# Seven block products in place of eight in three of four SwiGLU layers, and the whole state-space preparation beside the fourth

## Chip, cores and metric

The kernel runs on one core of one Trainium2 chip. The metric is the device time of one execution in microseconds (us), and the median of several executions is compared. Engines are named as in the profile: PE is TensorE's matmuls, PEld its weight loads, DVE VectorE, ACT ScalarE, POOL GpSimd, SP SyncE, which here only issues transfers.

## The reference

A trunk of two layers, each made of SwiGLU, token mixing, SwiGLU, runs over 640 tokens (512 latent, 128 context) with a model width of 1024. The token mixing of layer 0 is attention beside RWKV-7, that of layer 1 is a bidirectional S5. All of it is float32.

```python
D_MODEL, D_FF, DEPTH = 1024, 2816, 2
def swiglu(h, w1, w3, w2):
    return (jax.nn.silu(h @ w1) * (h @ w3)) @ w2
def run_trunk(x, mods, P, ctx):
    for l in range(DEPTH):
        h = modulated_in(x, P['norm_pre'][l, 0], m[:, 0])
        f = swiglu(h, P['ffn_w1'][l, 0], P['ffn_w3'][l, 0], P['ffn_w2'][l, 0])
        x = residual_out(x, f, P['norm_post'][l, 0], m[:, 0], 0.5)
        ...  # token mixing: attention and RWKV-7 (l = 0), S5 (l = 1)
        h = modulated_in(x, P['norm_pre'][l, 2], m[:, 2])
        f = swiglu(h, P['ffn_w1'][l, 1], P['ffn_w3'][l, 1], P['ffn_w2'][l, 1])
        x = residual_out(x, f, P['norm_post'][l, 2], m[:, 2], 0.5)
def modulated_in(x, gain, m):
    return rms_norm(x, gain) * (1 + m[:, None, 1]) + m[:, None, 0]
def residual_out(x, y, gain, m, weight):
    return x + weight * m[:, None, 2] * rms_norm(y, gain)
```

S5 also needs tables that depend on its parameters alone (powers of the poles, injection, read-out and Toeplitz matrices); computing them is the state-space preparation.

## The kernel before

Activations are held transposed: features on the partitions (8 tiles of 128), tokens along the row, in two halves of 320. Every float32 product is made of three matmuls on rounded operands: high weights by high activations, high weights by low activations, low weights by high activations (`mm3`, L439 to L441). So each weight tile is split on the chip into `whi` (ACT, L411) and `wlo = w - whi` (DVE, L412) after its load, and each activation tile into a high and a low part (`split`, L363 and L364).

There are four SwiGLU layers, named (layer, place): (0,0), (0,2), (1,0) and (1,2). Each runs `ffn`. Its 22 tiles of 128 hidden features go in six blocks (`FBLOCKS`: 4, 4, 4, 4, 2 and 4 tiles). Per block, the up part forms h @ w1 and h @ w3 for each tile and half (24 matmuls of 128x320 each), applies the gate on ACT and DVE (`th` L478 and L479, `g` L481) and splits the result into `gh` and `gl`; the down part then adds the block's share of all eight output tiles to `y` (L530, L532). In the first and the last block the two halves go one after the other, with their weights split twice, so that the norm of one half runs beside the matmuls of the other.

Between sublayers stand `post_norm` (sum of squares over the tiles, `ms` L335, `rr` on POOL L336, `diag` L340, a broadcast `ps_rb` L341, then `yr` L390 and `x` L393 on DVE) and the next `pre_norm` (the same chain, then `xr` L354 on DVE, `hh` L356 on ACT, `hl` L357 on DVE). For half 0 both are issued after its last down matmul; for half 1 the pre-norm waits until the next sublayer has begun (`flush`).

The preparation (`s5_prep`, 61 jobs) is put between the tiles of two SwiGLU layers as background work. A job of `s5_slice` loads its inputs over POOL's queue, makes twelve DVE products of 128x256 (L1488 to L1490, L1506 to L1508), lets PE transpose or multiply them, and stores the result over POOL's queue. The division is this:

```python
cut = 21 + 5 * 3
bg = {(0, 2): prep[:cut], (1, 0): prep[cut:]}
```

The order of the instructions of each engine is fixed when the kernel is built, by a scheduler that goes by the program's order and raised priorities; each engine then runs its list in order. PSUM has eight banks: three of a ring, one half of a wide tile that serves as every fourth of that ring, and four others.

## Time and profile before

| | us |
|---|---|
| median of 3 runs | 3202.66 (3195.01 to 3205.19) |
| the profiled execution, its own time | 3197.65 |
| span of that profile, first to last instruction | 3195.9 |
| PE busy in the span | 2949.9 |
| DVE, ACT, POOL busy | 1849.7, 1183.1, 711.3 |
| mean granted TensorE clock, share of 2.4 GHz | 0.949 |

A busy time is the sum of an engine's instructions. The views used below are the busy time by stretch (us from the span's start, per engine, with the number of instructions, then the granted clock), the list of an engine's instructions in order of time, and the groups of equal instructions.

### The profile page before, as it was taken

How to read it: one execution, taken by the hardware profiler on the slowest of the kernel's cores; microseconds unless marked ns; L12 is line 12 of the kernel's file. 1: busy time of each engine (PE TensorE's matmuls, PEld its weight loads, DVE VectorE, ACT ScalarE, POOL GpSimd, SP SyncE). 2: the span in 40 equal slices, each digit the busy share in tenths (PEclk: the TensorE clock that was granted, in tenths of full speed). 3: DMA queues.
4: the chain of work that ended last, by engine and by line, in shares of the span. 5: the costliest groups of instructions: out<-in, count | busy, mean ns of one | idle time of the engine just before them, and what ended most of it. 6: DMA issues, size and time to landing. Idle time of an engine off the chain costs nothing.

```text
span 3195.9 us, 57300 instructions
## 1 busy us (share of the span) xinstructions
PE 2949.9 (92%) x23107; PEld 2758.9 (86%) x23107; DVE 1849.7 (58%) x3775; ACT 1183.1 (37%) x2443; POOL 711.3 (22%) x844
## 2 busy tenths in 40 slices
PE   7999998997888788999999999999987699999998
PEld 6999998985666567999999989999986599999998
DVE  5433348524646654864675876665678846533346
ACT  4422235423444534533333542222452245422223
POOL 1000004024312201533231322232224624000002
PEclk8999999997788998999999999999988899999998
DMA  6433335541111107345444454453469653432223
GB/s 227 139 130 121 106 106 181 173 162 49 22 33 31 26 15 208 113 151 159 139 145 127 141 171 146 145 160 105 140 159 253 237 172 104 160 108 77 70 90 112
DMA packets 372302, 408.55 MB, mean 128 GB/s; under 512 B 75465, under 2 KB 338438, under 8 KB 371782
## 3 DMA queue, kind: packets, MB, share of 16 engines
q1 hardware_dynamic: 357542, 365.93, 37.1%
q0 software_dynamic: 14496, 38.97, 4.0%
q8 instruction: 182, 2.98, 0.4%
q14 instruction: 82, 0.67, 0.1%
HBM read 358.79 MB, written 44.86 MB: 126 GB/s over the span
## 4 chain that ended last, share of the span: by engine, by line
PE 79%; DVE 8%; DMA 4%; POOL 3%; ACT 2%; issue 2%; SPq 1%; POOLq 0%; DVEq 0%; ACTq 0%
PE ps_h L439 10%; PE ps_h L440 10%; PE ps_h L441 10%; PE ps_wide L439 6%; PE ps_wide L440 6%; PE ps_wide L441 6%; PE ps_y L439 5%; PE ps_y L440 5%; PE ps_y L441 5%; PE ps_wide L274 2%; DVE s5x L1633 1%; PE ps_in L439 1%; PE ps_in L441 1%; PE ps_in L440 1%; PE ps_n L84 1%
## 5 line engine op out<-in xcount | busy, mean ns | idle before, releaser
L411 ACT CAST whi<-w 128x1024 fp32r<-128x1024 f32 (+2 forms) x576 | 483.1, 846 | 852.9 <-PE ps_h L440 285.0
L412 DVE TENSOR_TENSOR wlo<-w,whi 128x1024 fp32r<-128x1024 f32 (+2 forms) x574 | 574.8, 1007 | 383.6 <-ACT whi L411 374.6
L439 PE MATMUL ps_h<-hh,whi 128*128 128x320 f32 x2112 | 658.2, 312 | 6.8 <-ACT whi L411 2.7
L440 PE MATMUL ps_h<-hl,whi 128*128 128x320 f32 x2112 | 657.3, 311 | 0.3 <-DVE hl L357 0.3
L441 PE MATMUL ps_h<-hh,wlo 128*128 128x320 f32 x2112 | 655.9, 311 | 0.0
L439 PEld LDWEIGHTS ps_h<-hh,whi 128*128 128x128 f32 x2112 | 399.3, 189 | 13.4 <-ACT whi L411 4.6
L440 PEld LDWEIGHTS ps_h<-hl,whi 128*128 128x128 f32 x2112 | 398.8, 189 | 2.8 <-issue 1.5
L441 PEld LDWEIGHTS ps_h<-hh,wlo 128*128 128x128 f32 x2112 | 398.6, 189 | 1.0 <-issue 0.8
L440 PE MATMUL ps_y<-gl,whi 128*128 128x320 f32 x1056 | 325.9, 310 | 0.0
L441 PE MATMUL ps_y<-gh,wlo 128*128 128x320 f32 x1056 | 325.4, 310 | 0.0
L439 PE MATMUL ps_y<-gh,whi 128*128 128x320 f32 x1056 | 323.5, 311 | 1.4 <-ACT y L530 1.3
L439 PE MATMUL ps_wide<-hh,whi 128*128 128x320 f32 x912 | 288.0, 316 | 7.3 <-ACT hh L363 4.4
L440 PE MATMUL ps_wide<-hl,whi 128*128 128x320 f32 x912 | 285.7, 313 | 0.7 <-DVE hl L357 0.7
L441 PE MATMUL ps_wide<-hh,wlo 128*128 128x320 f32 x912 | 284.7, 312 | 0.4 <-DVE wlo L412 0.4
L373 POOL TENSOR_TENSOR ssy<-ssy,sq 128x320 f32<-128x320 f32 x84 | 94.0, 1119 | 562.9 <-ACT sq L372 560.5
L439 PEld LDWEIGHTS ps_y<-gh,whi 128*128 128x128 f32 x1056 | 197.0, 188 | 6.7 <-ACT y L530 2.5
L440 PEld LDWEIGHTS ps_y<-gl,whi 128*128 128x128 f32 x1056 | 198.2, 188 | 0.9 <-issue 0.5
L441 PEld LDWEIGHTS ps_y<-gh,wlo 128*128 128x128 f32 x1056 | 198.0, 188 | 1.1 <-issue 0.8
L439 PEld LDWEIGHTS ps_wide<-hh,whi 128*128 128x128 f32 x912 | 173.6, 190 | 14.5 <-issue 5.3
L481 DVE SCALAR_TENSOR_TENSOR g<-th,ps_h 128x320 f32<-128x320 f32 x159 | 77.1, 485 | 175.1 <-PE ps_h L441 174.7
L440 PEld LDWEIGHTS ps_wide<-hl,whi 128*128 128x128 f32 x912 | 173.1, 190 | 3.3 <-issue 1.4
L441 PEld LDWEIGHTS ps_wide<-hh,wlo 128*128 128x128 f32 x912 | 172.9, 190 | 0.9 <-DVE wlo L412 0.6
(465 smaller groups left out, 5595.4 us busy)
## 6 DMA issues: line engine op xcount, KB each, us to landing
w<-in_ffn_w_dram SPq DMA_DIRECT2D x120, 1024.0 KB
ada_w<-in_ada_w_dram SPq DMA_DIRECT2D x72, 1024.0 KB
w<-in_ffn_w_dram SPq DMA_DIRECT2D x112, 512.0 KB
w<-in_ab_w_in_dram SPq DMA_DIRECT2D x14, 1024.0 KB
s5cd<-s_work POOLq DMA_DIRECT2D x128, 64.0 KB, 2.5
s5bd<-s_st POOLq DMA_DIRECT2D x32, 256.0 KB, 3.6
s5bt<-s5bd SPq DMA_DIRECT2D x32, 256.0 KB
w<-in_s_w_out_dram SPq DMA_DIRECT2D x8, 1024.0 KB
```

Source lines behind the costliest of these rows:

```text
L84: i = self.nc.tensor.matmul(**p).ins
L274: nc.tensor.matmul(ps[32 * g:32 * g + 32, :256], self.sc[:, 2 * t + k, :], w[:, k, g * 256:g * 256 + 256], start=(t + k == 0), stop=(2 * t ...
L373: nc.gpsimd.tensor_tensor(ss, ss, sq, op=OP.add)
L411: a = self.nc.scalar.copy(hi[:, :kt], s)
L412: v = (eng or self.nc.vector).tensor_tensor(lo[:, :kt], s, hi[:, :kt].bitcast(F32), op=OP.subtract)
L439: nc.tensor.matmul(o, hi[:, k], ah[k][half], start=(k == 0), stop=False)
L440: nc.tensor.matmul(o, hi[:, k], al[k][half], start=False, stop=False)
L441: self.last[0] = nc.tensor.matmul(o, lo[:, k], ah[k][half], start=False, stop=(k == kt - 1))
L481: nc.vector.scalar_tensor_tensor(g, t, 0.5, p3[:, :HALF], op0=OP.mult, op1=OP.mult)
L1633: V.tensor_tensor(dst, dst, t1, op=OP.add)
```

## The change

In (0,0), (1,0) and (1,2) the up part of all blocks but the first goes by seven block products. Two hidden tiles and two token halves make a product of 2x2 blocks with the contraction (8 tiles) halved, which takes eight block products in plain form; Winograd's form needs seven (12 matmuls each), of sums and differences of blocks. The sums on the activation side (`t1`, `t2`, `t4`, and half 1's first four tiles overwritten) are made once per layer by `block_inputs`; those on the weight side are made for each pair of tiles and each of w1 and w3, in float32 on POOL, by `sums` in `block_products`, and each of the seven weight blocks (128x512) is split on ACT and DVE. The products are combined on DVE from PSUM. A layer has 9 such pairs with two jobs each, so 54 jobs in all. The blocks become 4, 4, 4, 4, 4 and 2 tiles (`SBLOCKS`); half 1's down part of the last two blocks is joined. Since the new tiles need room, `x` is stored to DRAM before block 1 and loaded again in the last block. All 61 preparation jobs go to (0,2), which stays as it was otherwise.

```diff
+SBLOCKS = ((0, 4), (4, 8), (8, 12), (12, 16), (16, 20), (20, 22))
+    def block_inputs(self):
...
+        for k in range(4):
+            u, a = tmp(), tmp()
+            G(u, f(b12[1][k]), f(b11[1][k]), op=OP.subtract)
+            V(a, f(b12[0][k]), f(b11[0][k]), op=OP.subtract)
+            V(a, a, u, op=OP.add)
+            self.split(t1[0][k], t1[1][k], a)
...
+        return {1: b11, 2: b21, 3: b22, 4: t4, 5: t1, 6: t2, 7: b12}
+    def block_products(self, jobs, moving, pool):
...
+        def split2(m, *parts):
...
+                nc.scalar.copy(h, src)
+                v = nc.vector.tensor_tensor(l, src, h.bitcast(F32), op=OP.subtract)
...
+        def weights(m, stage):
+            if stage == 0:
...
+                def sums():
+                    G(s1, A(1, 0), A(1, 1), op=OP.add)
+                    G(A(1, 0), A(0, 0), A(1, 0), op=OP.subtract)
+                    G(A(0, 0), s1, A(0, 0), op=OP.subtract)
+                split2(m, (1, A(0, 0), sums), (6, A(0, 0), None))
+            elif stage == 1:
+                A = m["A"]
+                split2(m, (2, A(0, 1), lambda: G(A(0, 1), A(0, 1), A(0, 0), op=OP.subtract)), (5, m["s1"], None))
+                split2(m, (7, A(1, 0), None))
+            else:
+                A = m["A"]
+                split2(m, (4, A(1, 1), None), (3, A(0, 1), None))
...
+            if stage == 0:
+                m["X"], m["Y"] = self.ps("ps_x"), self.ps("ps_z")
+                x = prod(m, 1, m["X"], True, False)
...
+                nc.scalar.copy(m["p1"], x)
+                z = prod(m, 6, m["Y"], True, False)
...
+                V(m["u2"], m["p1"], z, op=OP.add)
+            elif stage == 1:
+                m["take"](0, prod(m, 2, m["X"], False, True))
+                m["W"] = self.ps("ps_w5")
+                w = prod(m, 5, m["W"], True, False)
+                z = prod(m, 7, m["Y"], False, False)
...
+            else:
+                z = prod(m, 4, m["Y"], False, True)
...
+                w = prod(m, 3, m["W"], False, True)
...
+                split_early(M[i + 1], 0)
+                split_early(m, 2)
+                split_early(M[i + 1], 1)
+                products(M[i + 1], 0)
+                products(m, 2)
+                products(M[i + 1], 1)
...
+        seven = not bg
+        self.g = self.open("g", 8 if seven else 10)
...
+            if seven and bi == 1:
+                self.spill_x()
+                self.close("res")
+                moving, pool = self.block_inputs(), self.open("blkt")
...
-        cut = 21 + 5 * 3
-        bg = {(0, 2): prep[:cut], (1, 0): prep[cut:]}
+        bg = {(0, 2): prep}
```

Three places in the order of the instructions show it. (Line numbers of the changed kernel are its own: L394 there is L393 before.)

DVE, at the passage from (0,2) to (1,0): `gl` is the last of (0,2), `ms` and `diag` belong to the pre-norm of half 0 of (1,0), and `xr` is the first product of that norm. Before:

```order
L364 TENSOR_TENSOR gl<-g,gh 128x320
L335 TENSOR_SCALAR ms<-ps_ms 128x3
L340 TENSOR_SCALAR diag<-ident,rr 128x128 x2
L340 TENSOR_SCALAR diag<-ident,rr 64x64
L532 TENSOR_TENSOR y_1_12951<-y_1_12951,ps_wide 128x320
L532 TENSOR_TENSOR y_1_12953<-y_1_12953,ps_y 128x320
L412 TENSOR_TENSOR wlo<-w,whi 128x512
L532 TENSOR_TENSOR y_1_12955<-y_1_12955,ps_y 128x320
L412 TENSOR_TENSOR wlo<-w,whi 128x512
L354 SCALAR_TENSOR_TENSOR xr<-x,mods_12946,ps_rb 128x320 x4
```

The last twelve rows up to the same `xr` now (`s_work` and `s_bc` are tiles of the preparation):

```order
L1677 TENSOR_TENSOR s_work<-s_bc,s_lp 128x256
L1676 TENSOR_TENSOR s_work<-s_bc,s_lp 128x256
L1678 TENSOR_TENSOR s_work<-s_work 128x256
L1677 TENSOR_TENSOR s_work<-s_bc,s_lp 128x256
L1678 TENSOR_TENSOR s_work<-s_work 128x256
L1694 TENSOR_TENSOR s_work<-s_bc,s_lp 128x2x16x8
L341 TENSOR_SCALAR diag<-ident,rr 128x128 x2
L1695 TENSOR_TENSOR s_work<-s_bc,s_lp 128x2x16x8
L341 TENSOR_SCALAR diag<-ident,rr 64x64
L1694 TENSOR_TENSOR s_work<-s_bc,s_lp 128x2x16x8
L1696 TENSOR_TENSOR s_work<-s_work 128x256
L1695 TENSOR_TENSOR s_work<-s_bc,s_lp 128x2x16x8
```

Between (0,2)'s last `gl` and the fourth `gl` of (1,0), DVE has 84 instructions before; now it has the same 84 and 101 of the preparation among them. Between the last `gl` of the last block's half 0 and that of its half 1 it has 56 before, now these and 49 of the preparation.

DVE, in the up part of block 2 of (0,0): before, each tile and half takes `th`, `g` and `gl`, and a few weight splits fall between.

```order
L479 SCALAR_TENSOR_TENSOR th<-th,ps_h_3881 128x320
L481 SCALAR_TENSOR_TENSOR g<-th,ps_wide 128x320
L364 TENSOR_TENSOR gl<-g,gh 128x320
L412 TENSOR_TENSOR wlo<-w,whi 128x256
L479 SCALAR_TENSOR_TENSOR th<-th,ps_h_3937 128x320
L481 SCALAR_TENSOR_TENSOR g<-th,ps_h_3938 128x320
```

Now (in a middle block of the same layer; `blk_p`, `blk_u`, `blk_v` and `blk_c` are partial sums of the products, `blk_g` the gate):

```order
L549 TENSOR_TENSOR blk_u<-blk_p,ps_wide 128x320
L503 TENSOR_TENSOR wlo<-w,whi 128x512 x4
L503 TENSOR_TENSOR wlo<-blk_s,whi 128x512
L634 SCALAR_TENSOR_TENSOR blk_g<-blk_g,ps_x 128x320
L556 TENSOR_TENSOR blk_v<-blk_p,ps_wide 128x320
L503 TENSOR_TENSOR wlo<-w,whi 128x512
L557 TENSOR_TENSOR blk_v<-blk_v,ps_w_4244 128x320
L634 SCALAR_TENSOR_TENSOR blk_g<-blk_g,blk_v 128x320
L549 TENSOR_TENSOR blk_u<-blk_p,ps_z 128x320
```

A job has seven splits and five sums that were not there, and its splits take in 3584 columns where two plain tiles took 2048.

POOL, in the same blocks: before it had no work there but the small sums of the modulation; now one job after the other has four sums of 128x512, of which this is one job and the next one's first sum.

```order
L515 TENSOR_TENSOR blk_s<-w 128x512
L516 TENSOR_TENSOR w<-w 128x4x128
L517 TENSOR_TENSOR w<-blk_s,w 128x4x128
L522 TENSOR_TENSOR w<-w 128x4x128
L515 TENSOR_TENSOR blk_s<-w 128x512
```

Over the whole program PE's matmul instructions go from 19,505 to 18,857, all of the difference 128x320; DVE's instructions go from 3,777 to 4,413 and POOL's from 849 to 1,098.

## Rows read from the trace of the kernel before

**Rows 1.** The page: span, and busy time of each engine.

```profile
span 3195.9 us, 57300 instructions
PE 2949.9 (92%) x23107; PEld 2758.9 (86%) x23107; DVE 1849.7 (58%) x3775; ACT 1183.1 (37%) x2443; POOL 711.3 (22%) x844
```

**Rows 2.** Busy time by stretch: in (0,2), at its end, after it, in (1,2).

```profile
core 0: us, PE busy (x) PEld busy (x) DVE busy (x) ACT busy (x) POOL busy (x), PEclk, DMA share, GB/s
1760.00:1840.00 80.00, 80.00 (x550) 79.44 (x549) 69.35 (x129) 42.84 (x78) 29.03 (x27) 1.00 0.42 131
1840.00:1920.00 80.00, 73.94 (x504) 71.17 (x503) 57.22 (x125) 38.76 (x84) 15.48 (x25) 0.96 0.54 170
2880.00:2960.00 80.00, 80.00 (x548) 80.00 (x547) 31.68 (x54) 18.76 (x31) 0.00 (x0) 1.00 0.20 63
```

**Rows 3.** PE in order of time in (0,0): first and last of 36 matmuls.

```profile
469.76 0.31 PE L439 MATMUL ps_h<-hh,whi 128*128 128x320 f32 x1
...
474.90 0.31 PE L441 MATMUL ps_y<-gh,wlo 128*128 128x320 f32 x1
```

**Rows 4.** DVE in order of time; the `gl` that end groups of four.

```profile
1705.35 0.48 DVE L364 TENSOR_TENSOR gl<-g,gh 128x320 fp32r<-128x320 f32 x1
...
1748.76 0.48 DVE L364 TENSOR_TENSOR gl<-g,gh 128x320 fp32r<-128x320 f32 x1
...
1792.66 0.48 DVE L364 TENSOR_TENSOR gl<-g,gh 128x320 fp32r<-128x320 f32 x1
...
1839.61 1.11 DVE L364 TENSOR_TENSOR gl<-g,gh 128x320 fp32r<-128x320 f32 x1 [0.53 <-ACT gh L363]
...
1894.92 0.48 DVE L364 TENSOR_TENSOR gl<-g,gh 128x320 fp32r<-128x320 f32 x1
```

**Rows 5.** DVE in order of time, back to back: start, us, engine, line.

```profile
1796.88 0.48 DVE L532 TENSOR_TENSOR y<-y,ps_y 128x320 f32<-128x320 f32 x1
1797.27 0.68 DVE L412 TENSOR_TENSOR wlo<-w,whi 128x512 fp32r<-128x512 f32 x1
1797.88 0.48 DVE L532 TENSOR_TENSOR y<-y,ps_y 128x320 f32<-128x320 f32 x1
...
1848.52 0.42 DVE L1488 TENSOR_TENSOR s_work<-s_bc,s_lp 128x256 f32<-128x256 f32 x1
1848.86 0.42 DVE L1489 TENSOR_TENSOR s_work<-s_bc,s_lp 128x256 f32<-128x256 f32 x1
1849.19 0.60 DVE L1506 TENSOR_TENSOR s_work<-s_bc,s_lp 128x256 f32<-128x256 f32 x1
1849.63 0.62 DVE L1507 TENSOR_TENSOR s_work<-s_bc,s_lp 128x256 f32<-128x256 f32 x1
```

**Rows 6.** Groups of DVE and POOL: count, busy, mean ns, idle before.

```profile
L1488 DVE TENSOR_TENSOR s_work<-s_bc,s_lp 128x256 f32<-128x256 f32 x64 | 27.0, 421 | 17.6 <-DMA s_bc<-s5bc 14.9 <-DMA s5cd<-s_work 1.7 <-PE ps_s5b L1493 0.4
L857 POOL TENSOR_TENSOR rope<-att_q,k_cos 128x512 f32<-128x512 f32 x4 | 5.1, 1272 | 10.2 <-ACT att_q L794 10.2
L1848 POOL TENSOR_TENSOR s5z<-hh,hl 128x320 f32<-128x320 f32 x16 | 15.2, 950 | 36.4 <-DVE glu L1850 36.4
```

**Rows 7.** DVE and POOL side by side in the S5 scan, in order of time.

```profile
2473.10 0.81 DVE L1633 TENSOR_TENSOR s5x<-s5x,sj 128x640 f32<-128x640 f32 x1
2473.83 1.91 DVE L1632 TENSOR_TENSOR sj<-sj,sj 128x640 f32<-128x640 f32 x1
...
2473.16 1.90 POOL L1628 TENSOR_TENSOR sj<-s5x,s_a 128x656 f32<-128x656 f32 x1
```

**Rows 8.** PE at the passage from (0,0) to (0,1): waits over 1 us.

```profile
554.83 0.63 PE L439 MATMUL ps_in<-hh,whi 128*128 128x320 f32 x1 [8.19 <-ACT pm L767]
570.43 1.81 PE L341 MATMUL ps_rb<-diag,ones 128*128 128x128 f32 x6 [2.04 <-DVE diag L340]
573.52 0.90 PE L439 MATMUL ps_in<-hh,whi 128*128 128x320 f32 x2 [1.29 <-ACT hh L356]
```

**Rows 9.** Transfers of `x`: queue, count, KB each, median us from issue to landing.

```profile
xd<-x POOLq DMA_DIRECT2D x2, 2560.0 KB, 8.9
```

**Rows 10.** Busy time by stretch at the passage from (0,0), columns as in rows 2.

```profile
550.00:555.00 5.00, 0.17 (x1) 0.17 (x2) 5.00 (x14) 2.13 (x7) 3.74 (x3) 0.50 1.03 304
570.00:575.00 5.00, 3.24 (x10) 2.46 (x10) 3.46 (x14) 2.28 (x8) 0.28 (x2) 0.50 0.61 210
```

More of the change, by code (lines that the diff above doesn't have):

```diff
@@ L482, in up, with up_pairs, gate, close @@
             self.split(gh[half], gl[half], g)
+        def up_pairs(f0, gh, gl):
+            jobs = []
+            for p in range(len(gh) // 2):
+                c = slice((f0 + 2 * p) * 128, (f0 + 2 * p + 2) * 128)
+                ts = {}
+                def gate(n, v, ts=ts):
+                    t = ts[n] = pool.tile([128, HALF], F32, name="blk_g", bufs=5)
+                    nc.scalar.activation(t, v, AF.Tanh, scale=0.5)
+                    nc.vector.scalar_tensor_tensor(t, t, 1.0, v, op0=OP.add, op1=OP.mult)
+                def close(n, v, ts=ts, p=p):
+                    t = ts[n]
+                    nc.vector.scalar_tensor_tensor(t, t, 0.5, v, op0=OP.mult, op1=OP.mult)
+                    self.split(gh[2 * p + n // 2][n % 2], gl[2 * p + n // 2][n % 2], t)
+                for w, take in ((w1, gate), (w3, close)):
+                    jobs.append((lambda w=w, c=c: self.wload(w[:, c], KT, 256), take))
+            return self.block_products(jobs, moving, pool)
         bg, slots = list(bg), FBLOCKS[-1][0] - FBLOCKS[0][1]
@@ L494, in background @@
             slots -= 1
[L496 removed]
+        blocks = SBLOCKS if seven else FBLOCKS
+        kept = None
+        for bi, (f0, f1) in enumerate(blocks):
             nb = f1 - f0
[L498 to L500 removed]
+            gh, gl = [[[] for _ in range(nb)] for _ in range(2)]
+            for g, tag in ((gh, "gh"), (gl, "gl")):
+                for _ in range(2):
+                    for i in range(nb):
+                        g[i].append(self.g.tile([128, HALF], F32R, name=tag, tag=tag))
+            first, last = bi == 0, bi == len(blocks) - 1
+            keep = seven and bi == len(blocks) - 2
             ssy = [None, None]
@@ L505, in ffn @@
                 ssy = [self.small.tile([128, HALF], F32, name=f"ssy{h}", bufs=1) for h in range(2)]
-            for hs in (((0,), (1,)) if first or last else ((0, 1),)):
-                for i in range(nb):
+            if seven and bi == 1:
+                self.spill_x()
+                self.close("res")
+                moving, pool = self.block_inputs(), self.open("blkt")
+            if seven and not first:
+                for n, _ in enumerate(up_pairs(f0, gh, gl)):
+                    if n and not last:
+                        background()
+            if seven and last:
+                self.close("blkt", "blk")
+                self.res = self.open("res", 1, "right")
+                self.new_x()
+                for half in range(2):
+                    c = slice(half * HALF, (half + 1) * HALF)
+                    nc.gpsimd.dma_start(self.xt[:, :, c], self.xd[:, :, c])
+            for hs in ((0,),) if keep else ((0,), (1,)) if first or last else ((0, 1),):
+                if kept and hs == (1,):
+                    f0, nb, gh, gl = kept[0], f1 - kept[0], kept[1] + gh, kept[2] + gl
+                for i in range(nb if first or not seven else 0):
                     with ExitStack() as c:
@@ L1898, in run @@
                 self.ffn(l, j, on_half, fill, bg.get((l, j), ()))
-                if prep and (l, j) == (1, 0):
+                if prep and (l, j) == (0, 2):
                     self.close("s5k")
```

78 lines of the change are left out of this document (73 added, 5 removed).

## The prediction

> **What bounds the kernel now.** I read the page first: PE is busy 2949.9 us of a span of 3195.9, DVE 1849.7, POOL 711.3 [rows 1]. Then the stretches: inside the SwiGLU layers PE has no idle time at all, and in (1,2) DVE needs only 31.68 of 80 us and POOL nothing [rows 2]. A matmul is listed with 0.31 us because they are pipelined; what counts is the pitch, (474.90 - 469.76) / 35 = 0.147 us [rows 3]. So there a matmul that is not issued returns 0.147 us, as long as no other engine becomes the bound. Two other readings matter. In the last part of (0,2) DVE is busy 69.35 and POOL 29.03 of 80 us and PE still never waits; in the stretch after it, with the passage to (1,0), PE is down to 73.94 [rows 2]. Other engines may be loaded far within a layer, and are the bound at a passage, where PE waits for the norms.
>
> **Matmuls removed.** 54 jobs with 84 matmuls in place of 96 are 648 fewer, which is the count in the order too. 648 x 0.147 = **-95 us**. PE itself gets nothing new to do.
>
> **The up parts of the block products.** Prices by the distance of one start to the next: a DVE product of 128x320 takes 0.40 us, a split of 128x512 0.61 (1796.88, 1797.27, 1797.88) [rows 5]. Four jobs, a block of four tiles, have 28 splits (17.1 us), 20 sums, 16 gate products and 8 low parts (44 x 0.40 = 17.6): 34.7 us of DVE. POOL has 16 sums at 1.27 us, by the row of the same size (5.1 us for four) [rows 6]: 20.3. PE needs 336 x 0.147 = 49.4 us. Each engine alone fits. But the two do not run freely side by side. In the S5 scan a DVE product of 128x640 with both operands in SBUF takes 0.81 us; the next begins at 2473.83 while POOL's runs until 2475.06, and ends at 2475.74, after 1.91 us [rows 7]: it waited until POOL was done and then took its usual time. 28 + 18 of the DVE instructions here have both operands in SBUF; the others read PSUM. If DVE and POOL took turns throughout, an up part would take 34.7 + 20.3 = 55.0 us, 5.6 more than PE, and 54 jobs 13.5 x 5.6 = 76 us. The other end is 0: the down part that follows has 28 us of matmuls and only 8 x 0.61 + 16 x 0.40 = 11.3 us of DVE, the order places the next block's first splits and POOL sums in it, and so the whole block asks for 66.3 of 77.6 us. The nearest row is the stretch in (0,2): 69.35 + 29.03 = 98 us of DVE and POOL in 80 without a wait of PE [rows 2]. That is a heavier load than here, but with looser dates. In the new form a PSUM bank is written again 24 matmuls (3.5 us) after its last product, so a DVE queue held up by two or three POOL sums is felt. I take **+20 us** (0.4 a job), bounds 0 and 76.
>
> The Trainium skill (SBUF — State Buffer, "Who interferes with whom") gives that waiting as a rule: a VectorE instruction with two SBUF inputs and a GpSimd instruction that reads SBUF share a port pair, held for the whole instruction. Rows 7 agree, with 1.91 us against 0.81. By the rule taken in full the sum ends at the first rival's time below; the row of (0,2) speaks for less.
>
> **The preparation beside (0,2).** PE does the same small products as before, elsewhere; DVE is what counts. A product of the preparation costs 0.34 us, one that reads in steps 0.44 (1848.52, 1848.86; 1849.19, 1849.63) [rows 5]. Between the last `gl` of (0,2) and the fourth of (1,0) stand the same 84 instructions as before and 101 of the preparation: 61 x 0.34 + 32 x 0.44 + 8 small ones = 36 us. Before, that stretch lasted from 1792.66 to 1839.61, 47 us [rows 4]; the 84 take about 37 (44 of 128x320, 8 splits of 128x512, 8 of double size, 24 smaller), so 10 us of idle time can take up a part: +26. The stretch ahead of it lasted 43.9 us (1748.76 to 1792.66) with some 30 us of work, and gets 49 more, 17 us: +3. The one after (to 1894.92) lasted 55, loses 17 instructions of the preparation, and gains 26 of the activation sums: 0. The one before both (1705.35 to 1748.76) stays inside its 43: 0. The stall has a place: the first matmul of (1,0) waits for `hh`, which waits for `xr`, and ahead of `xr` DVE now has 27 us of its list after the last `gl`, where PE has only half 1's down part, 96 x 0.147 = 14 us. So PE should wait some 15 us there, and about as much again within block 0. DVE in order also waits for the loads of the preparation (17.6 us in 64 cases before [rows 6], 0.3 us each). I take **+33 us**. Bounds: 24, if the preparation's DVE work comes into idle time after all, and 45, if every slice waits for its load and TensorE's clock is at 0.50 after the wait, as in the stretches from 550 and 570 [rows 10].
>
> **The activation sums.** Per layer 48 DVE products (19 us) and 8 on POOL at up to 0.95 [rows 6], beside the 576 matmuls (85 us) of block 0. They fit, closely in (1,2), where the second half's norm falls into the same 42 us. **+3 us**, 0 to 10. The store of `x` ahead of them takes about 9 us [rows 9] under the same block.
>
> **The last block.** Half 0's norms had 288 matmuls of half 1 as cover (42 us), now 144 (21 us). Ahead of the next sublayer's first matmul DVE has, beside `yr`, `x` and `xr`, eight `y` sums and eight splits of 128x768 (about 0.9 us each, by 0.61 for 512): some 20 us, and with the waits for `ms`, `rr` and `ps_rb` about 29 us after half 0's last product. PE would wait 8 to 10 us there. But it loses as much now, later: 8.19 + 2.04 + 1.29 us and a spell at a clock of 0.50, at the passage from (0,0), before half 1 can begin [rows 8, 10]; with half 0 later, half 1's norm is ready when its turn comes. **0**, from -8 to +15 for both passages. After (1,2) nothing follows but the output. The load of `x`, half of 2560 KB in half of 8.9 us [rows 9], begins when the last product is done and is needed some 15 us later: hidden, else 5 us a layer, inside that bound.
>
> **The sum.** 3197.65 (the profiled execution's own time) - 95 + 20 + 33 + 3 + 0 = 3158.65. The median of the runs shown is 5.0 us above that execution, so **3164 us**.
>
> **The rivals.** The forecast, a gain of 20 to 60 us, has a chance of 0.48.
> *DVE and POOL take turns in the up parts.* All 76 us are paid: 3202.66 - 95 + 76 + 33 + 3 = 3220, slower. It decides from 1.1 us of PE wait per job (59 us of 95 - 33 - 3). For it speak rows 7; against it the stretch in (0,2) and the work that lies in the down parts. 0.15.
> *Nothing is paid in the up parts* and the preparation costs its lower bound: 3202.66 - 95 + 24 = 3132. For it speaks the same stretch of (0,2). 0.25.
> *The passage costs twice as much.* PE's list there has the preparation's transposes between half 1's down part and the first product of (1,0), each waiting for DVE, which waits for loads issued by POOL behind other waits; such a ring costs by its latencies, not by its work. 70 us in place of 33: 3202.66 - 95 + 20 + 70 + 3 = 3201, no change. Against it: with 45 instructions of the preparation after 1839.61 DVE waited little (55 us for some 43 of work) [rows 4]. 0.12.
> That the matmuls are not saved can't be: the order has them.
>
> **The range.** From 3124 (no up part cost, 24 for the preparation, 8 gained at the passages) to 3226 (the lock in full and a little of the passages). Beyond it, both up parts and passages at their upper bounds would give 3252. For the forecast alone: 3143 to 3183. Faster by over 0.3% (10 us, about what three runs of this kernel can tell): 0.48 + 0.25 = 0.73; within 0.3%: 0.12; slower: 0.15.
>
> **What would show it.** Right: (0,0), (1,0) and (1,2) shorter by about 25 us each (216 x 0.147 = 32 less 7), with waits of PE under 1 us at a time in the up parts; at the passage from (0,2) to (1,0) a PE wait of 10 us or more ended by `hh`, with DVE busy without a gap; POOL and DVE sums stretched to about twice in the up parts. Wrong: waits of PE on `ps_w`, `ps_z` or on weight splits of over 1 us per job (then the first rival), or a passage without a wait (then the second); or PE waits on weight loads, since an up part now frees a load buffer later, which no row here prices.

## The result, and the profile after

The changed kernel is slower: 3242.64 us (median of four, 3236.74 to 3244.68) against 3198.84 for the kernel before beside it, a ratio of 1.0137, 95% interval 1.0122 to 1.0152, or 44 us. The forecast was 3164, a gain, with a range to 3226. 95 us of matmuls went, so 139 us were lost elsewhere, not the forecast's 56.

First the page of the changed kernel, the lines of [rows 1]:

```profile
span 3241.1 us, 57517 instructions
PE 2903.3 (90%) x22459; PEld 2693.9 (83%) x22459; DVE 2205.1 (68%) x4411; ACT 1309.0 (40%) x2791; POOL 1081.9 (33%) x1093
```

PE is busy 47 us less, and the span is 45 us longer: PE waits 92 us more. That is two thirds of the 139 us. The rest is that PE's busy time fell by 47 us and not by 95: the mean granted clock fell from 0.949 to 0.928, and after its waits PE works for a while at 0.50, the lower of its two levels (1.2 GHz), where one matmul follows the other after 0.267 us (six steps from 496.24 to 497.84) and not after 0.147. An estimate, from PE's busy time and clock in every 20 us of both traces: PE was busy at the lower level for some 227 us before and 326 now, and the 99 us more are worth 99 x (1 - 0.147 / 0.267) = 45 us.

Busy time by stretch, with the columns of [rows 2]:

```profile
1760.00:1840.00 80.00, 72.65 (x554) 67.93 (x552) 77.89 (x152) 41.36 (x92) 48.98 (x61) 0.98 0.57 171
1840.00:1920.00 80.00, 56.54 (x386) 49.28 (x386) 71.60 (x163) 27.25 (x67) 47.58 (x72) 0.75 0.51 152
2880.00:2960.00 80.00, 78.95 (x564) 76.54 (x563) 54.62 (x93) 29.76 (x60) 27.09 (x21) 1.00 0.35 113
2960.00:3040.00 80.00, 80.00 (x548) 80.00 (x547) 56.97 (x101) 29.51 (x57) 24.65 (x17) 1.00 0.25 80
```

In the middle blocks of (1,2) PE has hardly a gap, and 548 matmuls in 80 us are still 0.146 us each. Most of what is lost is lost at the edges of the layers: at the end of (0,2) and after it PE is busy 72.65 and 56.54 us where it had 80.00 and 73.94, with the clock at 0.75 in place of 0.96. The stages, by the first product that the trace of each kernel shows in a bank of the sublayer (it can be a few us late; the kernels of the last four columns come below):

| us | before | changed | prep alone | plain last block | wide ring | last form |
|---|---|---|---|---|---|---|
| (0,0) from | 42.5 | 49.1 | 43.2 | 49.6 | 42.9 | 42.9 |
| (0,1) from | 530.7 | 528.3 | 531.4 | 521.9 | 531.1 | 516.6 |
| (0,2) from | 1299.6 | 1305.2 | 1297.0 | 1287.5 | 1302.3 | 1282.1 |
| (1,0) from | 1809.0 | 1855.9 | 1848.8 | 1840.5 | 1851.4 | 1838.4 |
| (1,1) from | 2331.5 | 2381.8 | 2382.6 | 2363.8 | 2343.8 | 2313.6 |
| (1,2) from | 2694.0 | 2754.9 | 2745.7 | 2729.1 | 2711.0 | 2676.3 |
| end | 3195.9 | 3241.1 | 3247.5 | 3214.5 | 3214.1 | 3159.5 |

Read as differences, the changed kernel starts 6.6 us late, gains 9.0 in (0,0) where 31.8 were taken out (216 x 0.147), loses 8.0 in (0,1), 41.3 in (0,2) and 10.6 in (1,1), and gains 15.7 in (1,2). (1,0) takes 3.4 more, with 31.8 us of matmuls and the work of 25 jobs taken out. One trace does not fix such a figure to a few us: (0,1), which no kernel here changes, took from 765.5 to 776.9 in these six, and from 760.4 to 780.0 in all the traces of this case.

The passage from (0,2) to (1,0), PE in order of time, some of its waits:

```profile
1835.05 0.44 PE L1681 MATMUL ps_s5b<-ident,s_work 128*128 128x128 f32 x2 [2.44 <-ACT s_t L1719]
1841.57 0.59 PE L1715 MATMUL ps_s5k<-s_work,s_bb 128*32 128x112 f32 x4 [2.27 <-DVE s_work L1696]
1845.74 0.69 PE L1681 MATMUL ps_s5b<-ident,s_work 128*128 128x128 f32 x2 [2.58 <-DVE s_t L1722]
1855.88 0.90 PE L440 MATMUL ps_h<-hh,whi 128*128 128x320 f32 x2 [1.61 <-ACT hh L357]
...
1898.35 0.69 PE L1681 MATMUL ps_s5b<-ident,s_work 128*128 128x128 f32 x2 [4.05 <-ACT s_st L1682]
1908.64 0.63 PE L441 MATMUL ps_y<-gl,whi 128*128 128x320 f32 x1 [4.26 <-DVE gl L365]
1929.85 1.44 PE L333 MATMUL ps_ms<-mean,ssx 128*128 128x1 f32 x6 [4.14 <-POOL ssx L374]
```

From 1832 to 1856 PE has nothing but preparation and the norm's small products, and stands idle for 14 us in all: each small product waits for the one before to come back through ACT or DVE. This repeats twice within block 0 of (1,0).

The end of (0,0) with the second half's norm of (0,1); at the first of these places ACT, the load of `x`, and the stretch around it; then the end of (1,0) with the passage to (1,1), and the end of (1,2):

```profile
492.63 1.44 PE L333 MATMUL ps_ms<-mean,ssy 128*128 128x1 f32 x6 [3.91 <-POOL ssy L374]
494.54 0.64 PE L440 MATMUL ps_y<-gh,whi 128*128 128x320 f32 x1 [0.47 <-ACT whi L412]
525.27 1.81 PE L342 MATMUL ps_rb<-diag,ones 128*128 128x128 f32 x6 [6.00 <-DVE diag L341]
557.52 0.83 PE L333 MATMUL ps_ms<-mean,ssx 128*128 128x1 f32 x6 [1.35 <-POOL ssx L374]
561.25 1.81 PE L342 MATMUL ps_rb<-diag,ones 128*128 128x128 f32 x6 [2.90 <-DVE diag L341]
564.34 0.64 PE L440 MATMUL ps_wide<-hh,whi 128*128 128x320 f32 x1 [1.28 <-ACT hh L357]
```

```profile
493.65 1.56 ACT L412 CAST whi<-w 128x768 fp32r<-128x768 f32 x2 [3.37 <-DMA w<-in_ffn_w_dram]
```

```profile
x<-xd POOLq DMA_DIRECT2D x2, 1280.0 KB, 9.0
```

```profile
478.00:496.00 18.00, 13.43 (x79) 12.28 (x78) 11.58 (x25) 7.97 (x19) 8.06 (x9) 0.87 0.85 276
```

```profile
2344.99 1.44 PE L333 MATMUL ps_ms<-mean,ssy 128*128 128x1 f32 x6 [3.92 <-POOL ssy L374]
2347.48 0.63 PE L440 MATMUL ps_wide<-gh,whi 128*128 128x320 f32 x1 [1.05 <-ACT whi L412]
2378.32 1.81 PE L342 MATMUL ps_rb<-diag,ones 128*128 128x128 f32 x6 [5.88 <-DVE diag L341]
2381.36 0.64 PE L440 MATMUL ps_wide<-hh,whi 128*128 128x320 f32 x1 [1.24 <-ACT hh L357]
2417.48 0.49 PE L342 MATMUL ps_rb<-diag,ones 128*128 128x128 f32 x2 [1.88 <-DVE diag L341]
2424.59 0.45 PE L1903 MATMUL ps_s5s<-ident,s_s0r 128*128 128x128 f32 x1 [6.62 <-DMA s_s0r<-in_state_s_dram]
2429.73 0.64 PE L440 MATMUL ps_wide<-hh,whi 128*128 128x320 f32 x1 [3.64 <-ACT hh L357]
...
3189.62 1.44 PE L333 MATMUL ps_ms<-mean,ssy 128*128 128x1 f32 x6 [3.92 <-POOL ssy L374]
3192.10 0.63 PE L440 MATMUL ps_wide<-gh,whi 128*128 128x320 f32 x1 [1.04 <-ACT whi L412]
```

Half 0's down part is done and half 1's cannot begin: its first weights (128x768, a larger load than the 128x256 of half 0) arrive while `x` is being loaded (the DMA share of these 18 us is 0.85), and PE stands at the norm's `ps_ms` first. How much of that wait is the load of `x` and how much the larger first load, no run parts. Then half 1's 144 matmuls are over before half 0 is ready for the next sublayer: 6.00 and 5.88 us.

At the passage from (1,0) the kernel before has only these waits, and at the one from (0,0) those of [rows 8]:

```profile
2363.46 1.44 PE L332 MATMUL ps_ms<-mean,ssx 128*128 128x1 f32 x6 [3.90 <-POOL ssx L373]
2366.43 1.84 PE L341 MATMUL ps_rb<-diag,ones 128*128 128x128 f32 x6 [1.54 <-DVE diag L340]
2369.56 0.63 PE L439 MATMUL ps_wide<-hh,whi 128*128 128x320 f32 x1 [0.88 <-ACT hh L356]
```

So 10.4 us at the end of (0,0) and 5.5 at the second half's norm stand in place of 11.5, and 24.2 in place of 6.3 at the passage from (1,0).

### The profile page after: what moved, and what is told of

It reads as the page before. It is cut to its first block, busy times and chain, and to the rows that moved or that the text cites. A ratio compares the mean times of both kernels' runs of the same rounds, so it can differ in the third digit from the quotient of the medians.

```text
span 3241.1 us, 57517 instructions
## 1 busy us (share of the span) xinstructions
PE 2903.3 (90%) x22459; PEld 2693.9 (83%) x22459; DVE 2205.1 (68%) x4411; ACT 1309.0 (40%) x2791; POOL 1081.9 (33%) x1093
## 5 line engine op out<-in xcount | busy, mean ns | idle before, releaser
L413 DVE TENSOR_TENSOR wlo<-w,whi 128x1024 fp32r<-128x1024 f32 (+3 forms) x442 | 424.1, 967 | 230.4 <-ACT whi L412 224.9
L412 ACT CAST whi<-w 128x1024 fp32r<-128x1024 f32 (+3 forms) x444 | 349.3, 797 | 454.2 <-PE ps_y L441 140.1
L503 DVE TENSOR_TENSOR wlo<-w,whi 128x512 fp32r<-128x512 f32 x324 | 268.6, 854 | 48.8 <-ACT whi L502 47.6
L502 ACT CAST whi<-w 128x512 fp32r<-128x512 f32 x324 | 192.2, 619 | 236.6 <-POOL w L517 70.7
L440 PE MATMUL ps_h<-hh,whi 128*128 128x320 f32 x816 | 257.3, 317 | 4.1 <-ACT hh L357 4.0
L441 PE MATMUL ps_h<-hl,whi 128*128 128x320 f32 x816 | 255.4, 314 | 0.5 <-DVE hl L358 0.3
L442 PE MATMUL ps_h<-hh,wlo 128*128 128x320 f32 x816 | 255.6, 314 | 0.1
L440 PEld LDWEIGHTS ps_h<-hh,whi 128*128 128x128 f32 x816 | 155.9, 192 | 7.1 <-ACT hh L357 4.7
L441 PEld LDWEIGHTS ps_h<-hl,whi 128*128 128x128 f32 x816 | 155.2, 190 | 3.4 <-DVE hl L358 1.7
L442 PEld LDWEIGHTS ps_h<-hh,wlo 128*128 128x128 f32 x816 | 155.2, 190 | 2.0 <-issue 1.6
```

Source lines behind the costliest of these rows:

```text
L412: a = self.nc.scalar.copy(hi[:, :kt], s)
L413: v = (eng or self.nc.vector).tensor_tensor(lo[:, :kt], s, hi[:, :kt].bitcast(F32), op=OP.subtract)
L440: nc.tensor.matmul(o, hi[:, k], ah[k][half], start=(k == 0), stop=False)
L441: nc.tensor.matmul(o, hi[:, k], al[k][half], start=False, stop=False)
L442: self.last[0] = nc.tensor.matmul(o, lo[:, k], ah[k][half], start=False, stop=(k == kt - 1))
L502: nc.scalar.copy(h, src)
```

## The experiments

Each stands with its median and the ratio to the kernel before on the same chip, [95% interval]; the changed kernel has 1.0137. The product of a ratio's distance and 3199 us is its loss.

**The preparation alone** (no block products).

```diff
-        seven = not bg
+        seven = False
```

> No block products at all (all layers in the plain form of the kernel before); only the 25 preparation jobs of (1,0) go to (0,2). Theory 1, a backlog: the stages (0,2) and (1,0) together lost about 82 us in the changed kernel (they are 50 us longer although 32 us of matmuls are gone), nearly all of it because DVE is still busy with the preparation when (0,2) ends; then this kernel alone loses 55 to 70 us, about 3260. Theory 2, the sum of the prediction: the preparation costs 33 us, about 3232, and the rest was lost by the block products. Theory 3, the two only hurt together (block 0 of (1,0) has to form its sums and the left-over preparation): under 25 us, about 3220.

3250.93, 1.0157 [1.0134, 1.0181]: 50 us lost, 52 by the medians. In size that is nearest to theory 1, a little under its 55. (0,2) is 42.4 us longer and (1,0) 11.3 longer without its 25 jobs, with no block product near.

**Two layers** ((0,0) and (1,2); the preparation divided as before).

```diff
-        bg = {(0, 2): prep}
+        cut = 21 + 5 * 3
+        bg = {(0, 2): prep[:cut], (1, 0): prep[cut:]}
...
-                if prep and (l, j) == (0, 2):
+                if prep and (l, j) == (1, 0):
                     self.close("s5k")
```

> Block products in (0,0) and (1,2) only; (1,0) is plain and the preparation is divided as in the kernel before. 432 matmuls fewer, 63 us at the full pitch. By the stages of the changed kernel: (0,0) and the next sublayer together gain about 7, (1,2) gains 16, the start of the program loses 6 if that is not chance: 3175 to 3185. By the prediction's sum (the up parts and the sums cost some 7 us a layer, passages nothing): 3150. If the block products cost as much as they save everywhere: 3199.

3190.52, 0.9976 [0.9961, 0.999]: a gain of 8 us where 63 were taken out, between the reading by stages and none at all. The block products lose most of their gain without the preparation near them.

**Ten tiles for the jobs.**

```diff
-        bg, slots = list(bg), FBLOCKS[-1][0] - FBLOCKS[0][1]
+        bg, slots = list(bg), FBLOCKS[-1][0] - FBLOCKS[0][1] - 4
```

> The changed kernel, with the 61 preparation jobs given out over the first 10 tiles of (0,2)'s middle blocks in place of 14 (7 and then 6 a tile for 5 and 4). If the passage to (1,0) lost its time to a backlog of DVE work, which has 15 to 25 us of room in each 40 us from 1400 to 1560 us of the changed kernel, most of it comes back: about 3195. If the preparation is paced by its own chain of transposes, copies and loads, whatever the place in the program, nothing changes: 3240. If the first slots then overload DVE in turn: 3225.

3237.08, 1.0111 [1.0084, 1.0138], not to be told from the changed kernel. The order explains it: the groups of `ps_s5k` stand at the same places of PE's list in both, so where they come was not set by the tile that asks for them. Their distance in the changed kernel is read from L1715 between 1590 and 1660 us (first and last start; eight matmuls a group):

```profile
L1715 PE MATMUL ps_s5k<-s_bc,s_bb x48: 182/183/203, 1592.3 to 1655.3; 128*32 128x16 f32 x48
```

Six groups, five steps in 63.0 us: 12.6 us a job, in a stretch where PE never waits. 32 such jobs need 400 us, and from the first, at 1558, to the end of (0,2), about 1832, there are 274.

**A plain last block** of four tiles in the three layers.

```diff
-        blocks = SBLOCKS if seven else FBLOCKS
+        blocks = FBLOCKS
...
-            keep = seven and bi == len(blocks) - 2
+            keep = False
...
-            if seven and not first:
+            if seven and not (first or last):
...
             if seven and last:
+                self.restore()
...
-                for i in range(nb if first or not seven else 0):
+                for i in range(nb if first or last or not seven else 0):
```

(`restore` forms again the block of activations that product 7 had replaced.)

> The changed kernel, but the last block of each of the three layers has four tiles in the plain form again (192 matmuls of up and 96 of down for each half), so that half 0's norms have 288 matmuls as cover. 144 matmuls come back, 21 us. If the short cover costs what the waits around the ends of the three layers and at the second half of the next sublayers add up to (about 35 us: some 8 after (0,0), 9 more in the second sublayer, 10 after (1,0), 8 in (1,2)), the sum is 14 us down: 3229. If the short cover costs nothing, as the prediction had it, 3264.

3213.39, 1.0039 [1.0019, 1.0058]: 31 us less than the changed kernel by the ratios (29 by the medians), though 144 matmuls, 21 us, came back. So the short last block cost 50 to 52 us (44 if the run with ten tiles stands for the changed kernel). Not all of it is cover: the run also has 12 of the 54 jobs less, and `restore` more, whose prices it does not part. PE's waits at the passage from (1,0), in place of the 24.2 us above:

```profile
2395.75 1.44 PE L333 MATMUL ps_ms<-mean,ssx 128*128 128x1 f32 x6 [3.90 <-POOL ssx L374]
2398.73 1.84 PE L342 MATMUL ps_rb<-diag,ones 128*128 128x128 f32 x6 [1.53 <-DVE diag L341]
2401.85 0.64 PE L440 MATMUL ps_wide<-hh,whi 128*128 128x320 f32 x1 [0.88 <-ACT hh L357]
```

At the passage from (0,0) the waits of [rows 8] are back, 8.19, 2.04 and 1.29, and no others over 1 us: 6.3 and 11.5 us, as in the kernel before.

**Two banks for the transposes** of a job in place of one, nine tiles, preparation alone (`seven = False` again).

```diff
-            ps = self.ps("ps_s5b", "pb")
+            ps = self.ps("ps_s5b", ("pb", "pn")[r])
...
-        bg, slots = list(bg), FBLOCKS[-1][0] - FBLOCKS[0][1]
+        bg, slots = list(bg), FBLOCKS[-1][0] - FBLOCKS[0][1] - 5
```

> No block products; the whole preparation in (0,2), as in the run with the preparation alone (52 us slower than before). Here the two transposes of a preparation job go to two PSUM tags in turn (pb with one bank, and pn with two) in place of pb alone, and the jobs are given out over 9 tiles in place of 14. Theory 1: the jobs were spaced some 12 us apart (one ps_s5k group each 12 us from 1550 to 1700 us) by the ring through the single bank, not by DVE's work, so that the last of them fell behind the end of (0,2); with the spacing at 7 to 9 us they end inside (0,2), and 30 to 45 of the 52 us come back: 3205 to 3220. Theory 2: what is short is DVE and POOL time in (0,2) as a whole; then PE waits inside the middle blocks instead, and the time stays near 3250.

3243.07, 1.0142 [1.0109, 1.0174]: 5 to 8 us back, not clear of the noise, and not 30. The stall has moved into the layer: one stretch, and what ACT waited for from 1664 to 1717 us:

```profile
1680.00:1720.00 40.00, 18.43 (x136) 12.17 (x136) 30.44 (x86) 8.98 (x33) 33.12 (x59) 0.50 0.50 127
```

```profile
ACT s_st L1682 <- DMA s5bd<-s_st: 26.2, 7, 5.3
```

Eight groups stand side by side in PE's list there. Each waits for the single buffer `s_st`, which is free when its store to memory has landed. Neither DVE (30.44 of 40) nor POOL (33.12) is full. So the second theory is not shown by that either: another part of the same ring (bank, buffer, store and load) is short.

**Two layers, plain last block, late store.**

```diff
-                self.spill_x()
+                with self.tc.issue_after(self.last_norm.ins):
+                    self.spill_x()
```

> Block products in (0,0) and (1,2) only, with the last block of four tiles plain in both, the preparation divided as in the kernel before, and the store of x behind the second norm of block 0 in place of at about 20 us. By the stages of the runs so far: 16 to 19 us gained in each of the two layers, nothing lost at the start: 3199 - 35 = 3164. If the start was slow for another reason, 6 more: 3170. If the gain of the plain last block was one of the passage (1,0) to S5 alone: 3190.

3178.89, 0.9944 [0.9925, 0.9963]: 18 us faster than before, half of the 35.

**All of it**: three layers, plain last block, late store, two banks.

> Block products in (0,0), (1,0) and (1,2) with a plain last block, the whole preparation in (0,2) with two banks and 9 tiles, and the late store of x: all that the theories ask for together. The run with the plain last block alone had 3213; less 6.6 for the store and 30 to 45 for the two banks: 3162 to 3177. If the two banks give nothing: 3207.

3208.8, 1.0034 [1.0019, 1.0049]: the plain last block's 3213 less the 6 us of the store, so the two banks gave nothing that shows, as alone.

**The late store alone**, in the changed kernel.

> The changed kernel, with only the store of x to memory held back in POOL's queue until the second norm of block 0 is done. In the changed kernel this store of 2560 KB is issued at about 20 us, beside the loads of the modulation weights, and the first product of (0,0) starts at 49.1 us in place of 42.5. If the store is the cause: start at 42 to 43 us, and 3236 in place of 3242 (or of 3237, as a program with the same order measured). If not: no change, and the start stays at 49.

3230.43, 1.0103 [1.0073, 1.0133], with the start at 43.1. When POOL issues the store, in the changed kernel and here (first and last start), and PE's first product:

```profile
L301 POOL DMA_DIRECT2D xd<-x x1: 732/732/732, 18.6 to 18.6; - x1
```

```profile
49.13 0.90 PE L440 MATMUL ps_h<-hh,whi 128*128 128x320 f32 x2 [2.41 <-ACT hh L357]
```

```profile
L301 POOL DMA_DIRECT2D xd<-x x1: 765/765/765, 56.5 to 56.5; - x1
```

```profile
43.11 0.90 PE L440 MATMUL ps_h<-hh,whi 128*128 128x320 f32 x2 [2.40 <-ACT hh L357]
```

The 6.0 us are what the store cost at the start: it lies beside the loads of the modulation weights, for which the first norm waits. By the ratios the whole kernel gained 11; the 5 beyond the start are not clear of the noise.

**A loose ring**, preparation alone: as with two banks, 11 tiles, and

```diff
-        bc = sp.tile([128, 4, NP * 16], F32, name="s5_bc", bufs=2)
+        bc = sp.tile([128, 4, NP * 16], F32, name="s5_bc", bufs=3)
...
-        st = sp.tile([128, 2, NP, 128], F32, name="s5_st", bufs=1)
+        st = sp.tile([128, 2, NP, 128], F32, name="s5_st", bufs=2)
...
-        ps = self.ps("ps_s5c", "pb")
+        ps = self.ps("ps_s5c", "pn")
```

> No block products, the whole preparation in (0,2). Every part of the preparation's ring is loosened: two PSUM tags for the transposes, two buffers s_st in place of one, three s_bc in place of two, jobs over 11 tiles. In the order no two ps_s5k groups stand side by side until the last pair (in the run with two banks alone eight of them stood behind one another, and PE waited 28 us there while ACT waited 26 us for the one s_st to be stored). If that ring is the price of the preparation: 3205 to 3215. If DVE and POOL lack the time, 12 DVE products and five DMA issues of POOL a job beside the layer's own splits and gates, PE waits elsewhere: 3235 to 3250.

3234.86, 1.0121 [1.0095, 1.0148]. By the numbers the second reading, but not by the trace. The jobs now run inside the layer with few waits, and then PE stands still:

```profile
1848.73 1.44 PE L333 MATMUL ps_ms<-mean,ssy 128*128 128x1 f32 x6 [4.02 <-POOL ssy L374]
1854.28 1.81 PE L342 MATMUL ps_rb<-diag,ones 128*128 128x128 f32 x6 [4.11 <-DVE diag L341]
1868.32 1.44 PE L333 MATMUL ps_ms<-mean,ssx 128*128 128x1 f32 x6 [12.23 <-POOL ssx L374]
```

These are half 0's norms. The transposes share the banks of the tag `pn` with them, and in the order the norm's first product now stands behind the last `ps_s5k` group.

**The wide ring**: as the loose one with 14 tiles, the banks of the norms left free by the last jobs, and the early loads on SP's queue.

```diff
-            ps = self.ps("ps_s5b", ("pb", "pn")[r])
+            ps = self.ps("ps_s5b", ("pb", "pn")[r if sl < 12 else 0])
...
-            nc.gpsimd.dma_start(rows[:, 64 * r:64 * r + 64],
+            nc.sync.dma_start(rows[:, 64 * r:64 * r + 64],
```

> No block products, the whole preparation in (0,2), with the loosened ring, but the last eight transposes' pairs stay off the bank of the norms (in the run with the loose ring the norms of half 0 came only after the last preparation job, and PE waited from 1844 to 1875 us), and the 16 early jobs load over SP's queue instead of POOL's, so that in the order they take 98 us of PE's work in place of 117 and the slices begin some 20 us earlier. If the 52 us were the lack of a place for 32 slices of 9 to 12 us each between 1550 and 1800: 3205 to 3220, with the norms of half 0 in time. If DVE and POOL are short however the jobs are queued: 3230 to 3245.

3207.84, 1.0045 [1.0028, 1.0062]: 14 us lost in place of 50, as the first reading had it. The distance of the groups (1500 to 1560 us), and the stretches of [rows 2]:

```profile
L1715 PE MATMUL ps_s5k<-s_bc,s_bb x40: 179/183/203, 1526.0 to 1558.3; 128*32 128x16 f32 x40
```

```profile
1760.00:1840.00 80.00, 74.38 (x559) 70.51 (x558) 77.61 (x149) 37.39 (x84) 42.67 (x60) 0.98 0.54 164
1840.00:1920.00 80.00, 73.86 (x480) 72.28 (x479) 63.12 (x131) 41.50 (x81) 24.19 (x27) 0.91 0.41 128
```

8.1 us a job here (11 to 15 from 1753 us on, where the transposes keep to one bank), and after 1840 PE is busy 73.86, as in the kernel before. The first group also starts at 1526.0, where the preparation alone had 1546.5, since the early jobs load over another queue (the loose ring, without that, had 1548). Bank, buffers, queue and the norms' banks were changed together here; the runs on the way, with 5 to 8 and 11 to 16 us back, say only that the first steps were not enough.

**The sums left out, and the sums moved.** The two-layer form again, for reference; without POOL's weight sums; without any sums; with the weight sums on DVE:

```diff
-                    G(s1, A(1, 0), A(1, 1), op=OP.add)
-                    G(A(1, 0), A(0, 0), A(1, 0), op=OP.subtract)
-                    G(A(0, 0), s1, A(0, 0), op=OP.subtract)
+                    V(s1, A(1, 0), A(1, 1), op=OP.add)
+                    V(A(1, 0), A(0, 0), A(1, 0), op=OP.subtract)
+                    V(A(0, 0), s1, A(0, 0), op=OP.subtract)
```

(and so the fourth, of `A(0, 1)`).

> The kernel with block products in (0,0) and (1,2), a plain last block and the late store once more, beside the two kernels below: 3179 expected.

> That kernel without POOL's four sums of weight blocks per job (products 1, 2, 5 and 7 take unsummed blocks, so this part of the computation is left out). If DVE and POOL take turns in the up parts at the price of the prediction's first rival (1.4 us a job, 28 jobs): 39 us less, 3140. At the price of its sum (0.4 a job): 11 less, 3168. By PE's windows of 80.00 in 80 us in the middle blocks, nearly nothing: 3174 to 3179.

> As the one without weight sums, and also without the sums of activations ahead of block 1 and their return ahead of the last block (the products take unsummed blocks). By the prediction's 3 us a layer: 6 less than that one. By PE's waits about block 1 of (0,0) and (1,2) in the changed kernel (1.2, 1.5, 1.4 and 1.1 us): 3 to 5 less. If the sums and the lock cost nothing and the layers still gain only 16 of 25 us each, something else eats the rest: no change.

> The two-layer form (block products in (0,0) and (1,2), plain last block, late store; 3180) with the four sums of weight blocks per job on DVE in place of POOL. Without any such sums it had 3163. If those 17 us are DVE and POOL holding each other up: about 3165 to 3172, since DVE has room (some 46 of 78 us a block, and 10 more for the sums). If they are the longer chain from load to split to product, wherever the sums run: 3178 to 3182. If DVE is then the bound of the up part: 3190.

3181.25, 0.9956 [0.994, 0.9971]; without weight sums 3163.01, 0.9898 [0.9874, 0.9923]; without any 3154.6, 0.9874 [0.9845, 0.9902]; with the weight sums on DVE 3163.64, 0.9904 [0.9881, 0.9926]. So with the weight sums on POOL the two-layer form is 17 to 19 us slower than without them, and nearly all of it comes back when DVE does them. DVE needs 0.69 us for such a sum where POOL took 1.35 to 1.61, so a job's chain of four sums is also 3 us shorter there: how much is that and how much the two engines beside one another, these runs do not part.

It is not a price per job. Counted from the first product of (1,2), PE's 450th instruction comes 1.2 us earlier with the sums on DVE, its 900th 6.5 and its 2400th 6.2: most of the difference arises where block 1 begins, and in the 1500 instructions between, the middle blocks, POOL's sums cost nothing. Both kernels from 2930 to 2970 us, on POOL and on DVE:

```profile
2930.00:2970.00 40.00, 40.00 (x275) 40.00 (x274) 24.46 (x43) 14.78 (x28) 16.14 (x12) 1.00 0.30 93
```

```profile
2930.00:2970.00 40.00, 40.00 (x274) 40.00 (x274) 32.69 (x62) 17.46 (x34) 0.00 (x0) 1.00 0.14 46
```

In (0,0) the two stay within 2.1 us of each other throughout. The profiled executions are 11.0 us apart, and 7.2 of them lie in (1,2).

The sums of activations and their return cost 8 us in two layers by the medians, which the intervals do not separate from nothing; in the traces (0,0) is the same without them and (1,2) 4.7 us shorter. Without any sums (1,2) lasts 475.8 us in place of 501.9 (first product to the end): 26.1 us for the 168 matmuls that it has fewer, 24.7 at 0.147 each. The unit of the gain was right.

**The same in the changed kernel.**

> The changed kernel with nothing but its four weight sums per job on DVE in place of POOL. The two-layer form gained 11 (the profiled executions) to 17 us (the medians) by this for 28 jobs, 0.4 to 0.6 a job; 54 jobs: 21 to 32 us, 3207 to 3218 against 3237 to 3243. If DVE, which is full at the passage from (0,2) and beside block 1 of (1,0), then delays those: 3225 or more.

3220.3, 1.0092 [1.0067, 1.0118]: 14 us (ratios) to 22 us (medians) back. The traces place some 11 of them: (1,0) is 5.4 us shorter and (1,2) 5.8, (0,0) the same within 1.4. Again most of it is at the beginning of block 1, some in the last block. In (1,0) PE has waits there in the changed kernel that are gone here, the longest of them this one:

```profile
2003.50 0.61 PE L534 MATMUL ps_z<-t2h,whi 128*128 128x320 f32 x1 [3.09 <-DVE blk_g L634]
```

From the 900th to the 2400th instruction of PE in (1,2) the distance of the two kernels stays at 2.9 us. The splits of 128x512 in the changed kernel and here (count, busy, mean ns, idle before), and one of POOL's sums in the changed kernel:

```profile
L503 DVE TENSOR_TENSOR wlo<-w,whi 128x512 fp32r<-128x512 f32 x324 | 268.6, 854 | 48.8 <-ACT whi L502 47.6
```

```profile
L503 DVE TENSOR_TENSOR wlo<-w,whi 128x512 fp32r<-128x512 f32 x324 | 218.9, 688 | 50.7 <-ACT whi L502 44.4 <-PE ps_z L535 1.9 <-PE ps_z L536 0.7
```

```profile
L522 POOL TENSOR_TENSOR w<-w 128x512 f32<-128x512 f32 x54 | 87.0, 1611 | 205.0 <-DVE wlo L503 204.7
```

The same instruction takes 0.854 us beside POOL and 0.688 without. POOL's four sums took from 1.350 to 1.611, where [rows 6] gave 1.272, and the same four on DVE 0.684 to 0.689.

**Together**: three layers with the wide ring, plain last block and late store; the same with the weight sums on DVE; and with the eight differences of activations there too.

> Block products in (0,0), (1,0) and (1,2) with plain last blocks, the late store, and the whole preparation in (0,2) as in the kernel above. The same with the narrow ring would be 3213 less 7 for the store, 3206. If the wide ring gives back 30 of the 52 us: 3176, level with the two-layer form at 3180. If it gives back 15: 3190.

> The three-layer form with the wide preparation ring and the sums on DVE: the gain of the sums (0 to 12 in two layers) by three halves on top of the kernel before last: 3160 to 3190.

> The three-layer form with the wide preparation ring, late store, plain last blocks and weight sums on DVE (3162), and also the eight differences of activations per layer on DVE: no work of the block products is left on POOL. The sums of activations, with their return, were worth some 8 us in two layers; if POOL's part of it is a third: 3157 to 3160; if DVE is full at block 1: 3162 to 3166.

3181.97, 0.9959 [0.9937, 0.9982]; 3161.63, 0.989 [0.9857, 0.9922]; 3160.97, 0.9895 [0.9881, 0.991]. The last form is 34 us faster than the kernel before and beats the changed one by 77 (0.9895 against 1.0137, of 3199). The two-layer form with the sums on DVE, 0.9904, cannot be told from it. The differences of activations gave nothing that shows.

## Why the prediction was wrong

**The last block** is the step that failed most. The prediction put it at 0, "from -8 to +15 for both passages", because "with half 0 later, half 1's norm is ready when its turn comes". The plain last block measured 44 to 52 us for it (with the 12 jobs in that figure). The wait of 8 to 10 us at half 0's norm was foreseen, and came with 6.00 and 5.88. What it was set against did not hold: at the passage from (0,0) the 8.19 us are gone, but 5.5 of the 11.5 are left, and at the passage from (1,0) there were never more than 6.3 to give up. And these were not in it: half 1's down part waits for its own weights, whose loads lie beside that of `x`, called hidden (3.91 and 0.47, 3.92 and 1.05); the wait comes in (1,2) as well (3.92 and 1.04), "after (1,2) nothing follows but the output" notwithstanding; and at the passage from (1,0) the second half's norm is late again (3.64 us, behind 6.62 for a load of the S5 state at 2425 us, both gone with the plain last block). I had counted DVE's work against 21 us of matmuls and no time for the loads. With these waits the changed kernel stands idle some 27 us longer at the three places than with the plain last block (4.4, 17.9 and 5.0); the rest of the 44 to 52, lower clock after the waits and the 12 jobs among it, is not placed.

**The preparation** had the right place and the right sign: DVE is full (77.89 of 80), PE waits at the passage and twice within block 0, and the first product waits for `hh`. The size was wrong: +33 (24 to 45) against 50 to 52. The step that failed was to price it by DVE's work in four stretches. What set it was the ring of bank, buffers and queue, at 12.6 us a job where DVE's work is about 4.5 (12 products at 0.34 to 0.44): so the jobs came too late, whatever tile asked for them. The third rival said this ("such a ring costs by its latencies, not by its work") and held 0.12; what spoke against it, 55 us for 43 of work, was one place where the ring happened not to be pressed. With the ring widened and begun earlier the same work costs 14 us: less than the 24 that I took for the least.

**The up parts** came near their size, partly by luck: +20 for 54 jobs, against 14 to 22 for the weight sums in the changed kernel, and 17 to 19 for 28 jobs in the two-layer form, where 0.4 us a job would be 11. The price was spread over all jobs, and the traces have most of it at the beginning of block 1, with nothing in the middle blocks. The first rival's mechanism is there, its price of 76 is not; in the middle blocks the second rival, "Nothing is paid in the up parts", was right. That the down part takes up the delay, as the prediction argued, fits this and was not tested. The rule of the Trainium skill (SBUF — State Buffer, "Who interferes with whom") that two-input VectorE instructions and GpSimd's reads exclude one another agrees with the splits, 0.854 against 0.688 us; taken as a bound on the whole up part it overstates.

**The store of `x`** was seen (about 9 us "under the same block") and put in the wrong place: it was issued at 18.6 us, beside the first loads, and cost 6.

**The activation sums**, +3 (0 to 10), cost at most 8 in two layers, with a return that the changed kernel does not have.

**The clock** was priced in one place, the upper bound of the preparation. By the estimate above, matmuls at the lower level are some 45 of the 139 us that the changed kernel lost; they are part of the other figures.

**The sum**, with what was measured: -95 + 51 (preparation) + 48 (last block) + 18 (weight sums) + 6 (store) + 12 at most (activation sums, 4 a layer) = +40, against +44. That it comes so close is in part luck: the parts were measured in different kernels and overlap at the passages, and the 12 jobs that the plain last block took out stand in both the 48 and the 18. The prediction's 3252 for up parts and passages at their upper bounds does not come out of its terms either: 3202.66 - 95 + 76 + 45 + 10 + 15 is 3254. The measured 3243 lies between that and its range.

Of what was to show it, the waits under about 1 us in the up parts came true but at the beginning of block 1 (1.48 and 3.09 us in (1,0), 1.36 in (1,2)). The stall of 10 us or more came in pieces: 14 us between 1832 and 1856, of which only the last 1.61 was ended by `hh`. Of the three layers none came to its 25 us; (1,2) was the nearest, with 15.7. DVE's splits did not stretch to twice their time, but to 1.24 times (0.854 by 0.688).

## What to carry to other kernels

A shorter program part on the bound engine is also a shorter cover: before cutting matmuls, list what each stretch of them hides (norms, the loads of the next weights, a reload), because the 144 matmuls (21 us) that the last blocks saved cost 44 to 52 us. Background work is priced by the slowest ring it goes round (buffers, bank, queue), not by its instructions; measure the distance of two jobs where nothing presses, multiply, and compare with the room. A price per job, too, is to be looked for in the trace: here the sums on POOL cost nothing where the blocks run evenly, and most of their price where the layer changes from one form of work to the other.

## What was not expected of the hardware

Moving four sums of 128x512 per job from POOL to an already busier DVE made the kernel faster by 14 to 22 us: a split took 0.854 us beside POOL's sums and 0.688 without them, and a sum 0.69 on DVE and 1.35 to 1.61 on POOL. And a stall costs more than its idle time: in the stretch from 1680 to 1720 us of the kernel with two banks PE's clock was 0.50 (the lower of its two levels, 1.2 GHz) after PE had been waiting on small transposes since 1664, and DVE, ACT and POOL were all idle for part of it; at the passage of the changed kernel the clock was 0.75 over 80 us, and over the whole kernel the slower matmuls are some 45 us more than before by the estimate above, half as much as the 92 us of waiting.
